# Loads, stores and gate pieces around band attention in a one-core encoder layer: pinned loads in fewer transfers, o and its reciprocals by pairs of heads, gate stores by ScalarE

## The chip, the cores and the metric

The kernel runs on one core of a Trainium2 chip. The metric is the device time of one execution in microseconds (us); lower is better. A core has five engines with instruction streams of their own: TensorE (PE), VectorE (DVE), ScalarE (ACT), GpSimd (POOL) and SyncE (SP), and 16 DMA engines that move data between device memory and the on-chip memory. SP, ACT and POOL each have a queue on which they issue transfers.

## The reference

One layer of a streaming encoder, on 1024 prompt frames and 64 sample frames (1088 columns in all), everything in float32:

```python
proj = xn @ w_in                      # xn = rmsnorm(x); split into cb, cc, ch, q, k, v, ga, gb
cv, conv_state = causal_conv(cc * ch, conv_prefix, w_conv)
ya = (cb * cv) @ w_conv_out
s = einsum('bqhd,bkhd->bhqk', q, k) * HEAD_DIM ** -0.5      # own chunk and 8 chunks before
p = softmax(where(allowed, s + bias, NEG_INF))              # bias by clipped distance, per head
o = einsum('bhqk,bkhd->bqhd', p, v)
yb = o.reshape(B, L, ATT_DIM) @ w_attn_out
merged = sigmoid(ga) * ya + sigmoid(gb) * yb
x = x + merged @ w_out
x = x + (silu(rmsnorm(x) @ w1) * (rmsnorm(x) @ w3)) @ w2    # then a last rmsnorm
```

There are 8 heads of 64. The sample frames attend to 512 cached rows and themselves. New conv state, keys and values are outputs too.

## The kernel before, in words

Every float32 operand is split into a rounded high part and a low part, and a product is three matmuls: high by high, high by low, low by high. The layer runs in stages on TensorE: the projection (to about 377 us of the span), attention with some of the gate projections woven in (to about 555), the remaining gate pieces, the merge (ya, yb, the sigmoids), the output projection, and the feed-forward block. Between stages tensors go through device memory: `q_d`, `k_d` and `v_d` hold q, k and v by head with high and low parts, `ga_d` and `gb_d` the gates, `o_d` the two halves of the attention output before they are added, `rc_d` the reciprocals of the softmax sums, `u_d` the conv branch, `x21_d` a quarter of the normed input that the projection overwrites on chip.

Attention (`attention`, L1016) runs over 8 heads by 9 query tiles t (eight of 128 prompt frames, one of 64 sample frames). A step issues the scores of one tile, the transposes of the tile two steps back, and for pairs of tiles the products with v four steps back. Score tiles are [128, up to 640] in PSUM; VectorE adds the bias and takes the maximum, ScalarE takes the exponent, TensorE transposes, ScalarE and VectorE split into high and low.

Scores need, for a head, q with its high part in both halves of the partitions and likewise its low part (two tiles, L847), and k with high in partitions 0 to 63 and low in 64 to 127 (L851). `head_load` (L844) brings in q in four transfers of 64 partitions, k in four, the bias in four and v in one; `frames_load` (L867) the cached and sample keys `ks` in four and their values `vs` in two. All go out on SP's queue. In the text of the program `head_load(h + 1)` stands at tile 1 of head h and `frames_load(h + 1)` at tile 5, but the scheduler orders what is not pinned by readiness. q, k, v have two buffers, `ks` and `vs` one, the bias two halves of one tile.

`pinned` (L776) fixes the order of an engine's instructions as written. Before the change it is applied to TensorE's matmuls and transposes and to VectorE's and ScalarE's work in attention, not to SP's transfers.

Gates: half of the gate columns are projected here, 32 pieces of 24 matmuls (`gates`, L792). Six run ahead of attention (32 less `WITH` 16 and `BEHIND` 10), 16 are woven into it, 10 run behind it. `GATES` has eight row blocks, `PIECES` four column pieces; pieces 2 and 3 of a block need the quarter that is reloaded from `x21_d` (L1058). A finished piece is copied from PSUM by VectorE into one of two staging tiles and stored by POOL (L810, L811).

At a head's end, `combine` (L879) copies the two halves of p v, adds them on POOL and stores them at `o_d` (L895): 128 partitions go to 2 by 64 rows of device memory. The reciprocals go out at L992 and L996. Behind attention the merge loads the gates of its first row block, u in four blocks, and `o_d` and `rc_d` in four blocks k of two heads (L1067 to L1083); both `o_d` and `rc_d` are one tensor, so the first of these loads waits for the last head's stores. The reciprocals are spread over 64 partitions in two transfers a block.

Of the kernel before, what the change touches and what calls it, by code (L numbers as in the profile page):

```python
# [16 lines left out]
P = 128  # L17
# [20 lines left out]
WITH = 16  # L38
# [27 lines left out]
def encoder_kernel(ctx: ExitStack, tc: tile.TileContext, ins, outs):  # L66
# [33 lines left out]
    o_d = dr.tile([2, ATT, T], F32, name="o_d")  # L100
    rc_d = dr.tile([NH, T], F32, name="rc_d")
# [690 lines left out]
    def gates():  # L792

        kinds = itertools.chain(["att"] * (4 * len(GATES) - WITH - BEHIND), ["mm"] * WITH, turns)
        pieces = [(i, c) for cs in ((0, 1), (2, 3)) for i in range(2) for c in cs]
        pieces += [(i, c) for i in range(2, len(GATES)) for c in range(4)]
        w = {}
        for i, c in pieces:
# [9 lines left out]
            def out(ps=ps, nm=f"gst{i}_{c}", dst=(ga_d if g == "a" else gb_d)[m * P : (m + 1) * P, o : o + n], n=n):  # L808
                st = st_pool.tile([P, HN], F32, tag="st", name=nm)
                tt_copy(st[:, :n], ps[:, :n])  # L810
                nc.gpsimd.dma_start(dst, st[:, :n])  # L811
# [6 lines left out]
    given = [0, False]  # L818
# [24 lines left out]

    def head_load(h):  # L844
        q = []
        for l in range(2):
            qq = hd_pool.tile([P, T], F32R, tag=f"q{l}", name=f"qd{h}_{l}")  # L847
            for j in range(2):
                nc.sync.dma_start(qq[j * HD : (j + 1) * HD].bitcast(F32), q_d[h, :, l])
            q.append(qq)  # L850
        k = hd_pool.tile([P, TP], F32R, tag="k", name=f"kd{h}")  # L851
        v = hd_pool.tile([P, 8, P], F32R, tag="v", name=f"vd{h}")
        halves = [(slice(l * HD, (l + 1) * HD), k_d[h, :, l]) for l in range(2)]
        for e in range(2):
            for ls, src in halves:
                nc.sync.dma_start(k[ls, 512 * e : 512 * e + 512].bitcast(F32), src[:, 576 * e : 576 * e + 512])
# [3 lines left out]
        nc.sync.dma_start(b[:HD, 384:576], near[:HD, :192])  # L860
        nc.sync.dma_start(b[HD:, 384:], near[HD:, :256])
        nc.sync.dma_start(b[:HD, :384], far[:HD])
        nc.sync.dma_start(b[HD:, HD:384], far[HD:, HD:])
        nc.sync.dma_start(v.bitcast(F32), v_d[h, :, :8])
        heads[h] = [q, k, None, v, None, b]

    def frames_load(h):  # L867

        ks = hd_pool.tile([P, CACHE + TS], F32R, tag="ks", name=f"ksd{h}", bufs=1)
        vs = hd_pool.tile([P, 5, P], F32R, tag="vs", name=f"vsd{h}", bufs=1)  # L870
        for l in range(2):
            ls, src = slice(l * HD, (l + 1) * HD), k_d[h, :, l]
# [797 lines left out]
```

## Time and profile before

| | us |
|---|---|
| median of 3 runs | 1520.41 |
| lowest, highest | 1517.18, 1522.82 |
| profiled execution, own time | 1515.17 |
| its span | 1513.4 |
| PE, DVE, ACT, POOL busy | 1464.5, 974.9, 669.0, 186.7 |
| first and last head's first scores start | 396.82, 527.33 |

The span runs from the first to the last instruction of one profiled execution. A group's row has line, engine, operation, target and source tile, shapes, count, busy time and mean; a window's row the busy time of each engine in a stretch. In a row of transfers, KB is the size of one and the last number the median time from issue to landing. Names without numbers stand for all buffers of a tile: `qd` is a head's q tile, `kd` its k, `vd` its v, `ksd` and `vsd` the frames' keys and values, `bb` the bias, `co` the output staged for `o_d`, `gst` a staged gate piece, `g` its PSUM bank, `ob` and `r` the merge's output tiles, `rawp` weights. Lines of several helpers show as L777. q0 is POOL's queue of transfers, q1 SP's.

### The profile page before, as it was taken

How to read it: one execution, taken by the hardware profiler on the slowest of the kernel's cores; microseconds unless marked ns; L12 is line 12 of the kernel's file. 1: busy time of each engine (PE TensorE's matmuls, PEld its weight loads, DVE VectorE, ACT ScalarE, POOL GpSimd, SP SyncE). 2: the span in 40 equal slices, each digit the busy share in tenths (PEclk: the TensorE clock that was granted, in tenths of full speed). 3: DMA queues.
4: the chain of work that ended last, by engine and by line, in shares of the span. 5: the costliest groups of instructions: out<-in, count | busy, mean ns of one | idle time of the engine just before them, and what ended most of it. 6: DMA issues, size and time to landing. Idle time of an engine off the chain costs nothing.

```text
span 1513.4 us, 26409 instructions
## 1 busy us (share of the span) xinstructions
PE 1464.5 (97%) x10130; PEld 1371.1 (91%) x10130; DVE 974.9 (64%) x1815; ACT 669.0 (44%) x1359; POOL 186.7 (12%) x308
## 2 busy tenths in 40 slices
PE   6999999999999998999999999999999999999997
PEld 5799999999988898998888999999999998788886
DVE  6886465464466646763489677666666768857576
ACT  6654433333477761542256444444444445403123
POOL 1210010000265651000100011100001011000000
PEclk9999999999999999999999999999999999999999
DMA  7597523223889867554432434433344448767675
GB/s 232 182 310 241 194 72 108 79 86 135 253 189 200 211 193 235 147 171 148 130 132 84 143 130 157 148 134 119 122 149 157 143 172 314 244 220 229 228 259 202
DMA packets 162334, 264.90 MB, mean 175 GB/s; under 512 B 25536, under 2 KB 95360, under 8 KB 162080
## 3 DMA queue, kind: packets, MB, share of 16 engines
q1 hardware_dynamic: 132848, 196.00, 41.6%
q0 software_dynamic: 28208, 65.12, 12.8%
q10 hardware_dynamic: 1152, 2.10, 0.4%
q8 instruction: 80, 1.31, 0.4%
q14 instruction: 46, 0.38, 0.1%
HBM read 171.06 MB, written 91.92 MB: 174 GB/s over the span
## 4 chain that ended last, share of the span: by engine, by line
PE 63%; issue 20%; DMA 8%; DVE 4%; ACT 1%; SPq 1%; POOL 1%; POOLq 0%; DVEq 0%; ACTq 0%
PE Ab L239 8%; PE Aa L239 8%; PE A L1587 7%; PE Db L239 4%; PE Da L239 4%; PE D L1587 3%; PE Bb L239 2%; PE B L1587 2%; PE g L777 2%; PE Ba L239 2%; DMA kd<-k_d 2%; PE Ak L239 2%; PE Acc L239 2%; PE Ach L239 2%; PE Acb L239 2%
## 5 line engine op out<-in xcount | busy, mean ns | idle before, releaser
L1587 PE MATMUL A<-ring,ht 128*128 128x512 f32 x528 | 126.7, 393 | 3.9 <-ACT acc L1597 2.2
L1587 PEld LDWEIGHTS A<-ring,ht 128*128 128x128 f32 x528 | 98.8, 188 | 27.5 <-ACT acc L1597 3.5
L777 PE MATMUL g<-xn,whp 128*128 128x272 f32 x512 | 104.1, 294 | 2.1 <-DVE gst L777 1.1
L1306 POOL DMA_DIRECT2D h_d<-hq x77 | 41.0, 532 | 415.7 <-DVE hq L123 238.8
L122 ACT CAST ring<-w2r 128x512 fp32r<-128x512 f32 (+1 forms) x78 | 43.6, 587 | 103.7 <-PE A L1587 52.3
L122 ACT CAST hq<-sa 128x512 fp32r<-128x512 f32 x77 | 47.7, 619 | 85.0 <-DVE sa L1318 56.3
L777 PEld LDWEIGHTS g<-xn,whp 128*128 128x128 f32 x512 | 80.9, 188 | 3.8 <-DVE gst L777 1.3
L777 PE MATMUL g<-xn,wlp 128*128 128x272 f32 x256 | 74.6, 292 | 0.0
L123 DVE TENSOR_TENSOR hq<-sa,hq 128x512 fp32r<-128x512 f32 x77 | 53.1, 690 | 32.6 <-ACT hq L122 32.5
L777 DVE CUSTOM_DVE_ANT_0 p<-s,bb 128x640 f32<-128x640 f32 (+5 forms) x72 | 47.8, 664 | 35.7 <-PE s L777 21.5
L123 DVE TENSOR_TENSOR wla<-rawa,wha 128x512 fp32r<-128x512 f32 x56 | 38.5, 687 | 40.5 <-ACT wha L122 40.5
L1587 PE MATMUL D<-ring,ht 128*128 128x512 f32 x264 | 63.9, 393 | 0.2 <-ACT acc L1597 0.2
L239 PE MATMUL Aa<-tt,wha 128*128 128x272 f32 x352 | 58.9, 288 | 2.7 <-ACT tt L122 2.5
L1587 PEld LDWEIGHTS D<-ring,ht 128*128 128x128 f32 x264 | 49.5, 188 | 12.0 <-ACT acc L1597 0.6
L239 PE MATMUL Ab<-mg,whb 128*128 128x272 f32 x352 | 58.4, 288 | 0.0
L239 PE MATMUL Aa<-mg,wha 128*128 128x272 f32 x352 | 58.3, 288 | 0.0
L239 PE MATMUL Ab<-tt,whb 128*128 128x272 f32 x352 | 58.2, 287 | 0.0
L302 PE MATMUL yb<-ob,whp 128*128 128x272 f32 x256 | 50.8, 295 | 7.4 <-ACT ob L122 5.6
L122 ACT CAST wha<-rawa 128x512 fp32r<-128x512 f32 x56 | 34.8, 621 | 51.2 <-PE Ab L239 35.2
L123 DVE TENSOR_TENSOR ring<-w2r,ring 128x512 fp32r<-128x512 f32 (+1 forms) x78 | 49.1, 646 | 12.0 <-ACT ring L122 11.8
L239 PEld LDWEIGHTS Aa<-tt,wha 128*128 128x128 f32 x352 | 49.6, 188 | 3.4 <-ACT tt L122 2.9
L777 ACT ACTIVATE p<-p,mx 128x640 f32<-128x640 f32 (+5 forms) x72 | 51.0, 708 | 3.7 <-DVE mx L777 3.0
(542 smaller groups left out, 4312.1 us busy)
## 6 DMA issues: line engine op xcount, KB each, us to landing
h_d<-hq POOLq DMA_DIRECT2D x77, 512.0 KB, 3.4
ht<-h_d SPq DMA_DIRECT2D x154, 256.0 KB, 3.7
rawa<-in_w_ff SPq DMA_DIRECT2D x11, 1024.0 KB, 5.8
rawb<-in_w_ff SPq DMA_DIRECT2D x11, 1024.0 KB, 5.4
w2r<-in_w_ff SPq DMA_DIRECT2D x11, 1024.0 KB, 5.7
qd<-q_d SPq DMA_DIRECT2D x32, 272.0 KB, 7.4
ga<-ga_d SPq DMA_DIRECT2D x32, 136.0 KB, 2.6
gb<-gb_d SPq DMA_DIRECT2D x32, 136.0 KB, 2.4
```

Source lines behind the costliest of these rows:

```text
L122: act.copy(hi, src)
L123: vec.tensor_tensor(lo, src, hi.bitcast(F32), op=ALU.subtract)
L239: mm(t[:, j, :HN], w[:, k, :], x[p][:, l, k, j * HN : (j + 1) * HN], start=p in (1, 2, 7) and k == 0 and n == 0, stop=k == 3 and n == 2, s ...
L302: mm(out, l, r, start=k + j == 0, stop=k == kt - 1 and j == 2)
L777: return lambda *a, **kw: pin(f(*a, **kw))
L1306: nc.gpsimd.dma_start(h_d[p, c - 1], hq.rearrange("p i l t -> p (i l t)").bitcast(F32))
L1587: mm(t, ht[k][:, j, x], w[:, l], start=p in (1, 2, 7) and k == 0 and n == 0, stop=k == len(ks) - 1 and n == 2, skip_group_check=p in (6, 5 ...
```

## The change

Five things, all around attention:

- The heads' loads are pinned in the order of the program on SP's queue, and so is the reload from `x21_d`, which now stands between head 0's q, k and bias and its v.
- They are fewer: q is one tile [128, 2, 1088] loaded by one transfer whose source repeats the head's rows (step 0, count 2) for the two halves of the partitions; k is loaded in two transfers and `ks` in two, with high and low (step TK, count 2) as the outermost dimension of the source. `values_load` and `frame_values_load` stand apart: frames' keys of head h and q, k, bias of head h + 1 go at tile 1, frames' values of h and v of h + 1 at tile 5.
- `o_d` and `rc_d` are four tensors each, one for each pair of heads; the merge's loads of a pair and of u are interleaved, and a pair's reciprocals come in one transfer with the head (step T, count 2) outermost.
- Gate pieces behind attention are copied and stored by ScalarE.
- Four gate pieces go ahead of attention in place of six, 18 with it, and the first three row blocks give their pieces 0 and 1 first.

```diff
 C_CB, C_CC, C_CH, C_Q, C_K, C_V, C_GA, C_GB = 0, 512, 1024, 1536, 2048, 2560, 3072, 4096
-WITH = 16
+WITH = 18
 BEHIND = 10
...
     gb_d = dr.tile([D, T], F32, name="gb_d")
-    o_d = dr.tile([2, ATT, T], F32, name="o_d")
-    rc_d = dr.tile([NH, T], F32, name="rc_d")
+    o_d = [dr.tile([2, P, T], F32, name=f"o_d{k}") for k in range(4)]
+    rc_d = [dr.tile([2, T], F32, name=f"rc_d{k}") for k in range(4)]
...
         kinds = itertools.chain(["att"] * (4 * len(GATES) - WITH - BEHIND), ["mm"] * WITH, turns)
-        pieces = [(i, c) for cs in ((0, 1), (2, 3)) for i in range(2) for c in cs]
-        pieces += [(i, c) for i in range(2, len(GATES)) for c in range(4)]
+        pieces = [(i, c) for cs in ((0, 1), (2, 3)) for i in range(3) for c in cs]
+        pieces += [(i, c) for i in range(3, len(GATES)) for c in range(4)]
         w = {}
...
                 st = st_pool.tile([P, HN], F32, tag="st", name=nm)
-                tt_copy(st[:, :n], ps[:, :n])
-                nc.gpsimd.dma_start(dst, st[:, :n])
+                if behind[0]:
+                    act.copy(st[:, :n], ps[:, :n])
+                    nc.scalar.dma_start(dst, st[:, :n])
+                else:
+                    tt_copy(st[:, :n], ps[:, :n])
+                    nc.gpsimd.dma_start(dst, st[:, :n])
...
     gate_products = gates()
-    given = [0, False]
+    given, behind = [0, False], [False]
...
+    load_at = pinned(nc.sync.dma_start)
+
+    def rows_of(src, *ap):
+        return bass.AP(tensor=src.tensor, offset=src.offset, ap=[list(d) for d in ap])
+
     def head_load(h):
-        q = []
-        for l in range(2):
-            qq = hd_pool.tile([P, T], F32R, tag=f"q{l}", name=f"qd{h}_{l}")
-            for j in range(2):
-                nc.sync.dma_start(qq[j * HD : (j + 1) * HD].bitcast(F32), q_d[h, :, l])
-            q.append(qq)
-        k = hd_pool.tile([P, TP], F32R, tag="k", name=f"kd{h}")
-        v = hd_pool.tile([P, 8, P], F32R, tag="v", name=f"vd{h}")
-        halves = [(slice(l * HD, (l + 1) * HD), k_d[h, :, l]) for l in range(2)]
+        q = hd_pool.tile([P, 2, T], F32R, tag="q", name=f"qd{h}")
+        load_at(q.bitcast(F32), rows_of(q_d[h], (0, 2), (2 * T, HD), (T, 2), (1, T)))
+        k = hd_pool.tile([P, 2, 512], F32R, tag="k", name=f"kd{h}")
         for e in range(2):
-            for ls, src in halves:
-                nc.sync.dma_start(k[ls, 512 * e : 512 * e + 512].bitcast(F32), src[:, 576 * e : 576 * e + 512])
+            load_at(k[:, e].bitcast(F32), rows_of(k_d[h, :, 0, 576 * e :], (TK, 2), (2 * TK, HD), (1, 512)))
         b = bb[:, h % 2]
...
         far = bias_rows(h, 0, 384)
-        nc.sync.dma_start(b[:HD, 384:576], near[:HD, :192])
-        nc.sync.dma_start(b[HD:, 384:], near[HD:, :256])
-        nc.sync.dma_start(b[:HD, :384], far[:HD])
-        nc.sync.dma_start(b[HD:, HD:384], far[HD:, HD:])
-        nc.sync.dma_start(v.bitcast(F32), v_d[h, :, :8])
-        heads[h] = [q, k, None, v, None, b]
+        load_at(b[:HD, 384:576], near[:HD, :192])
+        load_at(b[HD:, 384:], near[HD:, :256])
+        load_at(b[:HD, :384], far[:HD])
+        load_at(b[HD:, HD:384], far[HD:, HD:])
+        heads[h] = [q, k.rearrange("p e t -> p (e t)"), None, None, None, b]
+
+    def values_load(h):
+        v = heads[h][3] = hd_pool.tile([P, 8, P], F32R, tag="v", name=f"vd{h}")
+        load_at(v.bitcast(F32), v_d[h, :, :8])
...
-        ks = hd_pool.tile([P, CACHE + TS], F32R, tag="ks", name=f"ksd{h}", bufs=1)
-        vs = hd_pool.tile([P, 5, P], F32R, tag="vs", name=f"vsd{h}", bufs=1)
-        for l in range(2):
-            ls, src = slice(l * HD, (l + 1) * HD), k_d[h, :, l]
-            nc.sync.dma_start(ks[ls, :CACHE].bitcast(F32), src[:, T:])
-            nc.sync.dma_start(ks[ls, CACHE:].bitcast(F32), src[:, 512:576])
-        nc.sync.dma_start(vs[:, :4].bitcast(F32), v_d[h, :, 8:12])
-        nc.sync.dma_start(vs[:TS, 4].bitcast(F32), v_d[h, :TS, 12])
-        heads[h][2], heads[h][4] = ks, vs
+        ks = heads[h][2] = hd_pool.tile([P, CACHE + TS], F32R, tag="ks", name=f"ksd{h}", bufs=1)
+        for c, src, n in ((0, k_d[h, :, 0, T:], CACHE), (CACHE, k_d[h, :, 0, 512:], TS)):
+            load_at(ks[:, c : c + n].bitcast(F32), rows_of(src, (TK, 2), (2 * TK, HD), (1, n)))
+
+    def frame_values_load(h):
+        vs = heads[h][4] = hd_pool.tile([P, 5, P], F32R, tag="vs", name=f"vsd{h}", bufs=1)
+        load_at(vs[:, :4].bitcast(F32), v_d[h, :, 8:12])
+        load_at(vs[:TS, 4].bitcast(F32), v_d[h, :TS, 12])
...
             pool_e.tensor_tensor(o[:, :n], a[:, 0, :n], a[:, 1, :n], op=ALU.add)
-            to = o_d[:, h * HD : (h + 1) * HD]
+            to = o_d[h // 2][:, h % 2 * HD : (h % 2 + 1) * HD]
             spans = [((tok if tok < 512 else HT + tok - 512), 0, n)]
...
                 mm_at(
-                    ps[:, i], q[l][:, q0 : q0 + r], k[:, k0 + i * w : k0 + i * w + w], start=l == 0, stop=l == 1
+                    ps[:, i], q[:, l, q0 : q0 + r], k[:, k0 + i * w : k0 + i * w + w], start=l == 0, stop=l == 1
                 )
...
                     nc.gpsimd.dma_start(
-                        rc_d[h, e * HT : e * HT + 512].rearrange("(t p) -> t p", p=P), rows[4 * e : 4 * e + 4]
+                        rc_d[h // 2][h % 2, e * HT : e * HT + 512].rearrange("(t p) -> t p", p=P), rows[4 * e : 4 * e + 4]
                     )
                     c = e * HT + 512
-                    nc.gpsimd.dma_start(rc_d[h : h + 1, c : c + 32], rows[8:9, 32 * e : 32 * e + 32])
+                    nc.gpsimd.dma_start(rc_d[h // 2][h % 2 : h % 2 + 1, c : c + 32], rows[8:9, 32 * e : 32 * e + 32])
...
                 h, t = order[i]
-                if t == 1 and h + 1 < NH:
-                    head_load(h + 1)
-                elif t == 5 and h + 1 < NH:
-                    frames_load(h + 1)
+                if t == 1:
+                    frames_load(h)
+                    if h + 1 < NH:
+                        head_load(h + 1)
+                elif t == 5:
+                    frame_values_load(h)
+                    if h + 1 < NH:
+                        values_load(h + 1)
                 done.append(scores(h, t))
...
     head_load(0)
-    frames_load(0)
-
-    nc.sync.dma_start(xn.t[0, 1].rearrange("p l k t -> p (l k) t").bitcast(F32), x21_d)
+
+    load_at(xn.t[0, 1].rearrange("p l k t -> p (l k) t").bitcast(F32), x21_d)
+    values_load(0)
     gate(24 * (4 * len(GATES) - WITH - BEHIND), False)
...
     sg = gates_in(0)
-    for k in range(4):
+
+    def o_load(k):
+        rc, o2 = (ob.t[:, l, k].bitcast(F32) for l in range(2))
+        r = mp.tile([P, T], F32, tag="rc", name=f"r{k}", bufs=2)
+        nc.sync.dma_start(r, o_d[k][0])
+        nc.sync.dma_start(o2, o_d[k][1])
+        nc.sync.dma_start(rc, rows_of(rc_d[k], (T, 2), (0, HD), (1, T)))
+        vec.tensor_tensor(r, r, o2, op=ALU.add)
+        vec.tensor_tensor(r, r, rc, op=ALU.mult)
+        split(ob.t[:, 0, k], ob.t[:, 1, k], r)
+
+    def u_load(k):
         f = u.t[:, 1, k].bitcast(F32)
...
         split(u.t[:, 0, k], u.t[:, 1, k], f)
-    for k in range(4):
-        rc, o2 = (ob.t[:, l, k].bitcast(F32) for l in range(2))
-        r = mp.tile([P, T], F32, tag="rc", name=f"r{k}", bufs=2)
-        nc.sync.dma_start(r, o_d[0, k * P : (k + 1) * P])
-        nc.sync.dma_start(o2, o_d[1, k * P : (k + 1) * P])
-        for j in range(2):
-            src = rc_d[2 * k + j]
-            nc.sync.dma_start(
-                rc[j * HD : (j + 1) * HD], bass.AP(tensor=src.tensor, offset=src.offset, ap=[[0, HD], [1, T]])
-            )
-        vec.tensor_tensor(r, r, o2, op=ALU.add)
-        vec.tensor_tensor(r, r, rc, op=ALU.mult)
-        split(ob.t[:, 0, k], ob.t[:, 1, k], r)
+
+    o_load(0)
+    u_load(0)
+    o_load(1)
+    for k in range(1, 4):
+        u_load(k)
+    o_load(2)
+    o_load(3)
+    behind[0] = True
     gate(24 * 4 * len(GATES), False)
```

## The prediction, made before the change was timed

> **What bounds the kernel now.** I read the page first (span, busy shares, chain), then a table by windows over the stage that the change touches, then the waits, and last the transfers of that stage. From the page:
>
> ```profile
> span 1513.4 us, 26409 instructions
> PE 1464.5 (97%) x10130; PEld 1371.1 (91%) x10130; DVE 974.9 (64%) x1815; ACT 669.0 (44%) x1359; POOL 186.7 (12%) x308
> PE 63%; issue 20%; DMA 8%; DVE 4%; ACT 1%; SPq 1%; POOL 1%; POOLq 0%; DVEq 0%; ACTq 0%
> ```
>
> TensorE is busy 97% of the span, so at most 49 us stand open in the whole kernel, and this change removes no matmul. The windows show attention (397 to 545), the gate pieces behind it (560 to 590) and the start of the merge (600 to 612). Columns: us, busy of PE, weight loads, DVE, ACT, POOL, granted clock, share of the 16 DMA engines, GB/s.
>
> ```profile
> 397.00:472.00 75.00, 69.39 (x499) 64.09 (x499) 50.04 (x125) 56.17 (x135) 39.03 (x57) 1.00 0.85 204
> 472.00:491.00 19.00, 18.27 (x131) 16.89 (x130) 11.73 (x30) 14.35 (x35) 10.84 (x16) 1.00 0.90 199
> 560.00:590.00 30.00, 30.00 (x241) 30.00 (x240) 15.17 (x20) 10.30 (x16) 6.23 (x11) 1.00 0.70 220
> 600.00:606.00 6.00, 1.12 (x8) 0.91 (x8) 2.58 (x2) 0.82 (x1) 0.00 (x0) 0.97 0.82 210
> 606.00:612.50 6.50, 6.12 (x25) 5.80 (x26) 6.19 (x14) 4.00 (x10) 0.00 (x0) 0.50 0.21 60
> ```
>
> In attention TensorE is nearly full, but so are the transfers: the DMA engines hold packets 85 to 90% of the time. Every head reloads its q, k, v and bias tiles while the head before runs, so this stage has two bounds that lie close together, and what the change does to the loads decides it. The waits tell what loads and stores cost today (us in total, times, longest):
>
> ```profile
> PE s L777 <- DMA kd<-k_d: 6.4, 5, 2.3
> PE yb L302 <- ACT ob L122: 5.6, 2, 5.2
> SPq L1074 <- DMA o_d<-co_s: 8.2, 1, 8.2
> DVE gst L777 <- DMA gb_d<-gst: 12.9, 5, 4.1
> ```
>
> **What the change can win.** Scores wait 6.4 us for k; an order that is fixed on SP's queue could take that to zero. The merge waits 5.6 us for ob, after which the clock is granted at 0.50 for 6.5 us (the last window), which is 3.2 us of work lost; o_d in one tensor for each pair of heads lets the first three pairs load before the last head has been stored (the 8.2 us), which could remove both. That is 15.2 us. ScalarE in place of VectorE and POOL for the 10 gate pieces behind attention takes away the 12.9 us in which VectorE waits for a staging buffer, but in 560 to 590 TensorE is busy 30.00 of 30 us: nothing gained there, and ScalarE, busy 10.30 of 30, has room for ten copies and issues. What is queued behind each on ScalarE are the next weight casts and the splits of u and ob. Two gate pieces that move from ahead of attention into it add no work; they cost the cover of the first head's loads, below.
>
> **What the change costs.** The merged loads have the same bytes, and here is the step on which I decide. Before, q came in four loads of 64 partitions each, k in four, the frames' keys in four. Now one load has a source access pattern whose outermost dimension is 2: (0,2) for q, which is the two copies, and (TK,2) for k and ks, which is hi and lo. The reciprocals of the merge get (T,2). The trace of before has one transfer with such a pattern, the o_d store at L895, whose target is 2 by 64 rows. The first two lines below are a stretch in which that store alone moves data on POOL's queue (q0); the next two a stretch with a h_d store on the same queue, 128 rows on both sides:
>
> ```profile
> DMA packets 66, 0.03 MB, mean 42 GB/s; under 512 B 58, under 2 KB 58, under 8 KB 66
> q0 software_dynamic: 66, 0.03, 17.0%
> ...
> DMA packets 162, 0.54 MB, mean 287 GB/s; under 512 B 14, under 2 KB 34, under 8 KB 162
> q0 software_dynamic: 142, 0.52, 90.3%
> ```
>
> 17.0% of 16 engines is 2.7 engines, against 14.4 for the h_d store: the 2 by 64 store runs at 42 GB/s on about two engines, with the other fourteen empty. I take the same for the four merged loads, on SP's queue. The nearest row is this store; it is another queue and a store, so that stays the largest doubt (rivals). The Trainium skill, page "DMA: Bandwidth & Descriptors", section "Why a DMA increments its semaphore by 16 and not by 1", states that on either kind of queue a transfer uses the largest number of engines up to 16 that divides the slowest dimension of both sides, and that on SP's and ACT's these are the lowest-numbered; the store agrees with its 42 GB/s, and no run here shows it for SP. The same page, in "Rules for kernel authors", also advises one transfer of 128 partitions in place of two of 64, which is what the change does, and by that rule alone the sum would be the first rival's.
>
> Sizes and times now. The loads (KB each, us to landing), and a stretch in which large loads alone fill all engines:
>
> ```profile
> qd<-q_d SPq DMA_DIRECT2D x32, 272.0 KB, 7.4
> kd<-k_d SPq DMA_DIRECT2D x32, 128.0 KB, 6.5
> ksd<-k_d SPq DMA_DIRECT2D x16, 128.0 KB, 7.5
> ksd<-k_d SPq DMA_DIRECT2D x16, 16.0 KB, 7.5
> rawp<-in_w_in SPq DMA_DIRECT2D x4, 1024.0 KB, 5.3
> xn<-x_d SPq DMA_DIRECT2D x1, 2176.0 KB, 10.2
> u<-u_d SPq DMA_DIRECT2D x4, 544.0 KB, 9.4
> r<-o_d SPq DMA_DIRECT2D x4, 544.0 KB, 4.6
> ob<-o_d SPq DMA_DIRECT2D x4, 544.0 KB, 6.8
> ob<-rc_d SPq DMA_DIRECT2D x8, 272.0 KB, 7.9
> ...
> DMA packets 324, 0.81 MB, mean 407 GB/s; under 512 B 122, under 2 KB 141, under 8 KB 324
> ```
>
> 407 GB/s over 16 is 25.4 GB/s for one engine; the store's 42 over two is 21. Both are kept as ends, and I take 25.4, since loads of 2 KB and more are what it was read from. For each head, one of the two engines then carries:
> - q: 4 x 272 KB = 1.114 MB, half of it 557 kB, 21.9 us
> - k: 4 x 128 KB = 0.524 MB, half 262 kB, 10.3 us
> - ks: 2 x (128 + 16) KB = 0.295 MB, half 147 kB, 5.8 us
> - its sixteenth of all else: window 472 to 491 is one head and moves 199 GB/s x 19 us = 3.78 MB; less the 1.93 MB above, 1.85 MB over 16 is 116 kB, 4.5 us
>
> The sum is 42.5 us for a head. A head lasts 18.6 us now: first scores of head 0 at 396.82, of head 7 at 527.33, a seventh of the difference.
>
> ```profile
> 377.85 0.52 PE L777 MATMUL g<-xn,whp 128*128 128x272 f32 x2 [1.03 <-ACT scr L531]
> 378.72 1.79 SPq L849 DMA_DIRECT2D qd<-q_d  x1
> 396.82 0.34 PE L777 MATMUL s<-kd,qd 128*128 128x128 f32 x2
> 527.33 0.42 PE L777 MATMUL s<-kd,qd 128*128 128x128 f32 x2 [1.74 <-DMA kd<-k_d]
> 555.65 2.35 SPq L1069 DMA_DIRECT2D u<-u_d  x4
> ```
>
> Buffers don't hide that: q, k and v have two, so head h+1's loads may go out a head ahead, but the two engines carry 42.5 us of packets for every head whatever the lead. The pinned order adds to it that everything behind q and k on the queue (bias, values, the gates' weights) has a sixteenth of its packets waiting on the same two engines, and TensorE, whose order is pinned too, can't go round a late score. So:
> - Head 0: 378.7, 1.8 to issue, 2.6 for the weight load in front (1024 KB over 16), 21.9 and 10.3: scores at 415.3, 18.5 later than now. The gate pieces ahead are four from 377.85 on, of 24 matmuls each; window 560 to 590 has 241 in 30.00 us, so 3.0 us a piece: they end near 390 and cover none of the stop.
> - Head 1: 42.5 more, and 5.5 for x21 (2176 KB over 16), which is pinned behind head 0's loads: 463.3.
> - Heads 2 to 7: 6 x 42.5, so head 7 at 718.3 in place of 527.3: plus 191.0 us. SP's waits for free buffers (scores of the head before, its values) lie inside the 42.5, as TensorE is then ahead of the loads.
> - Head 7's own work follows a long stop. Going by the 606 window it runs 6.5 us at half clock: plus 3.2. In the heads before it that loss is hidden by the loads.
> - The merge: uo opens at about 555.65 as now. One of the two engines carries half of the reciprocals' 8 x 272 KB, 1.114 MB, 43.9 us, and a sixteenth of 12 loads of 544 KB (u, r, o2), 16.4 us: all landed at 616.0. Then VectorE multiplies, ScalarE rounds and VectorE subtracts over 1088 columns, 2.1 times the 690, 619 and 690 ns of 512 columns in the two rows below, some 4 us: ob is whole at 620, where TensorE goes on at 606 now: plus 14 us. The gate pieces cover it up to about 590 only, and ya up to 596. The 15.2 us to be won are gone: the waits they sit in are replaced by longer ones.
>
> ```profile
> L122 ACT CAST hq<-sa 128x512 fp32r<-128x512 f32 x77 | 47.7, 619 | 85.0 <-DVE sa L1318 56.3
> L123 DVE TENSOR_TENSOR hq<-sa,hq 128x512 fp32r<-128x512 f32 x77 | 53.1, 690 | 32.6 <-ACT hq L122 32.5
> ```
>
> 191.0 + 3.2 + 14 = 208.2 us. The profiled execution took 1515.17 us (its span 1513.4) and lies 5.2 under the median of 1520.41; 1515.2 + 208.2 + 5.2 = 1729 us. With 21 GB/s for an engine the head costs 51.5 us and the whole comes to 1813; with all else hidden a head costs 38.0 and the whole comes to 1697. This case's own range is 1690 to 1800.
>
> **The rivals.**
> 1. *The merged loads spread over all 16 engines* as the 64-row loads do now. Then bytes and rate are as before, SP has seven issues fewer for each head, and the 15.2 us come in as far as the stops allow: 1515.2 - 15.2 + 5.2 = 1505 us, faster. For it: the store of 42 GB/s is on another queue, and no SP transfer of before has an outermost 2. Against it: the engines are handed out by the shape of the pattern in the one place where it can be seen. It decides as soon as a merged q load lands in under 10 us.
> 2. *Two engines, but another pair for each transfer.* Then q's 21.9 us set the pace alone, k and ks run beside it: with 18.6 us of lead and about 2 us to issue and land, some 5 us of stop for each of six heads, and 8 for head 0: 1515.2 + 38 + 5.2 = 1558 us, the merge unchanged. For it: two o_d stores that overlapped in the trace moved 66 GB/s together, as in this stretch:
>
> ```profile
> DMA packets 80, 0.10 MB, mean 66 GB/s; under 512 B 57, under 2 KB 57, under 8 KB 80
> q0 software_dynamic: 80, 0.10, 24.0%
> ```
>
> so POOL's stores can take different pairs. Against it: that is POOL's queue, whose descriptors POOL writes; for SP's queue no row shows a change of engines, and I give it little.
>
> **How the numbers follow.** My case 0.82, rival 1 0.13, rival 2 0.05. The range is my case's own, 1690 to 1800, which leaves out its tails and both rivals: a little under 2 in 10. About 0.5% is what a measurement of this kernel can tell from no change. Rival 1 is 1.0% faster, with little chance of ending within 0.5%: faster 0.12, same 0.01. Both others are slower: 0.87.
>
> **What would show it.** Right, if the merged q load takes over 20 us to land, the DMA engines' share in attention falls to about 0.3 while TensorE idles some 24 us in each head (released by the loads of q and k), heads start about 42 us apart, and the merge's reciprocals take more than 10 us each. Wrong, if q lands in about 7 us, the DMA share stays at 0.85, and heads stay 18 to 19 us apart; then rival 1 holds. Heads about 23 us apart would be rival 2. A price off in size alone would show as a head spacing between 38 and 52.

## The result and the profile after

| | before | after |
|---|---|---|
| median, us | 1520.99 (1517.18 to 1522.82, 5 runs) | 1763.76 (1761.54 to 1766.85, 5 runs) |
| ratio | | 1.160, 95% interval 1.158 to 1.162 |
| span of the profiled execution | 1513.4 | 1762.4 |
| first scores of heads 0, 1, 7 | 396.8, 413.3, 527.3 | 412.2, 463.2, 734.2 |
| last matmul of attention | 555.38 | 767.93 |

The change makes the kernel 16% slower, 243 us by the medians and 249.0 us by the two spans. From the page of the changed kernel, the span, TensorE's busy time, and three rows of the slices (each digit is the busy share of a fortieth of the span, in tenths; GB/s is left out):

```profile
span 1762.4 us, 26310 instructions
PE 1499.8 (85%) x10130; PEld 1402.3 (80%) x10130; DVE 972.4 (55%) x1805; ACT 672.7 (38%) x1369; POOL 180.8 (10%) x298
...
PE   7999999984454544493899999999999999899998
...
PEclk9999999996676767797899999999999999999999
DMA  7695432243222322354454433433334334875776
```

The same 10130 matmuls run, at 85% in place of 97%. A slice is 44 us, and the tenth to the seventeenth are attention: there TensorE is busy 40 to 50% at a clock of 0.6 to 0.7, and the DMA engines stand at 20 to 30%, where the windows of before had 85 to 90%. Both bounds of the stage stand idle together, so something holds it back by a part of a resource: here, as the transfers below show, by few of the sixteen engines. The groups (busy us, mean ns of one | idle us ahead of them and what ended it) show who waits:

```profile
L777 PE MATMUL s<-kd,qd 128*128 128x320 f32 (+2 forms) x192 | 43.4, 337 | 180.2 <-DMA kd<-k_d 180.2
L302 PE MATMUL ya<-u,whp 128*128 128x272 f32 x256 | 53.5, 303 | 18.6 <-ACT u L122 15.0 <-DVE u L123 2.1 <-ACT gst L811 1.5
L302 PE MATMUL yb<-ob,whp 128*128 128x272 f32 x256 | 52.3, 302 | 14.8 <-ACT ob L122 14.1 <-DVE ob L123 0.7
```

The wait for k was 6.4 us in all before; now it is 180.2, eight times, the longest 26.7. The timeline of TensorE in the changed kernel (start, us, [idle before <- releaser]) has the stops ahead of the first, second and last head, and the last matmul of attention:

```profile
412.25 0.66 PE L777 MATMUL s<-kd,qd 128*128 128x128 f32 x2 [20.51 <-DMA kd<-k_d]
463.24 0.66 PE L777 MATMUL s<-kd,qd 128*128 128x128 f32 x2 [26.67 <-DMA kd<-k_d]
...
734.23 0.66 PE L777 MATMUL s<-kd,qd 128*128 128x128 f32 x2 [22.28 <-DMA kd<-k_d]
...
767.93 0.28 PE L777 MATMUL pv<-ident,sm 128*9 128x128 f32 x1
```

From 412.25 to 734.23 are seven heads: 46.0 us each, where it was 18.6 (45.2 without the first of the seven steps, in which the reload from `x21_d` stands). In the kernel before, the last line's instruction stands here:

```profile
555.38 0.28 PE L777 MATMUL pv<-ident,sm 128*9 128x128 f32 x1
```

So the 249.0 us fall into three: up to head 7's first scores 734.2 - 527.3 = 206.9; head 7's own work (767.93 - 734.23) - (555.38 - 527.33) = 5.6; and all behind attention (1762.4 - 767.93) - (1513.4 - 555.38) = 36.4.

What holds the heads is seen in the transfers of the changed kernel while one q load runs (524.7 to 547.3; packets and MB, then SP's queue q1: packets, MB, share of 16 engines):

```profile
DMA packets 913, 1.58 MB, mean 70 GB/s; under 512 B 669, under 2 KB 677, under 8 KB 785
...
q1 hardware_dynamic: 131, 1.10, 12.0%
```

12.0% of sixteen engines is 1.92: as much as two engines that hardly rest, and fourteen with nothing from SP. They move 1.10 MB in 22.6 us, 48.7 GB/s, or 24.3 GB/s each. The loads go one after the other. In the head before, `ks` and q were both issued by 471.92; the first packet of q (8704 bytes, two rows) comes at 478.0, behind the last of `ks`. SP's queue while `ks` alone has packets (472 to 476.5), and while k alone has, behind q (548 to 551):

```profile
q1 hardware_dynamic: 107, 0.22, 12.6%
...
q1 hardware_dynamic: 73, 0.15, 13.0%
```

Again that is two engines' worth, in the first window with q waiting in line. The order of the queue alone doesn't make q wait: as soon as the bias, which has no count of 2, is issued behind k, it runs beside it, and from 551 to 553 SP's queue holds 47.1%. SP's own timeline around that load (start, us, operation) shows the second half of the story:

```profile
512.57 1.10 SPq L777 DMA_DIRECT2D ksd<-k_d  x2
513.71 1.67 SPq L777 DMA_DIRECT2D qd<-q_d  x1
515.43 29.52 SPq L777 DMA_DIRECT2D kd<-k_d  x2
545.04 5.84 SPq L777 DMA_DIRECT2D bb<-bias_d  x2
```

The two k loads take SP 29.52 us to issue, with no releaser named. In each of heads 1 to 7 these issues end 2.9 to 3.3 us before the last packet of q, whatever their length (23.0 to 29.5 us), so it looks as if SP stands until the two engines have drained most of q. The bias of the next head is issued only then, and VectorE's first work on the scores waits for it (195.8 us in seven waits, in the time in which TensorE waits for k).

In the merge the same thing happens once more, with the reciprocals. SP's issues there, VectorE's waits for the reciprocals (us in total, times, longest), ScalarE's casts behind the first and second reciprocals, and the stops of TensorE that follow:

```profile
777.20 0.32 SPq L1079 DMA_DIRECT2D r<-o_d  x1
...
779.06 0.53 SPq L1081 DMA_DIRECT2D ob<-rc_d  x1
779.64 0.73 SPq L1088 DMA_DIRECT2D u<-u_d  x1
...
783.87 1.16 SPq L1081 DMA_DIRECT2D ob<-rc_d  x1
789.62 10.77 SPq L1088 DMA_DIRECT2D u<-u_d  x3
```

```profile
DVE r L1083 <- DMA ob<-rc_d: 41.8, 4, 11.1
```

```profile
798.14 1.10 ACT L122 CAST ob<-r 128x1088 fp32r<-128x1088 f32 x1 [13.77 <-DVE r L1083]
...
815.19 1.10 ACT L122 CAST ob<-r 128x1088 fp32r<-128x1088 f32 x1 [6.97 <-DVE r L1083]
816.20 1.09 ACT L122 CAST u<-u 128x1088 fp32r<-128x1088 f32 x1
```

```profile
817.34 0.60 PE L302 MATMUL ya<-u,whp 128*128 128x272 f32 x1 [15.01 <-ACT u L122]
835.96 0.60 PE L302 MATMUL yb<-ob,whp 128*128 128x272 f32 x1 [7.26 <-ACT ob L122]
```

u's last three loads stand behind two pairs of o and reciprocals on SP's queue, and on ScalarE the cast of u's second block stands right behind that of ob's second block, which waits, by way of VectorE, for the second reciprocals. So ya, which needs no reciprocal at all, stops 15.01 us for u, and yb then 7.26 and 6.85.

### The profile page after: what moved, and what is told of

It is laid out like the page before. It is cut to its first block, busy times and chain, and to the rows that moved or that the text cites. A ratio compares the mean times of both kernels' runs of the same rounds, so it can differ in the third digit from the quotient of the medians.

```text
span 1762.4 us, 26310 instructions
## 1 busy us (share of the span) xinstructions
PE 1499.8 (85%) x10130; PEld 1402.3 (80%) x10130; DVE 972.4 (55%) x1805; ACT 672.7 (38%) x1369; POOL 180.8 (10%) x298
## 5 line engine op out<-in xcount | busy, mean ns | idle before, releaser
L777 PE MATMUL s<-kd,qd 128*128 128x320 f32 (+2 forms) x192 | 43.4, 337 | 180.2 <-DMA kd<-k_d 180.2
L777 DVE CUSTOM_DVE_ANT_0 p<-s,bb 128x640 f32<-128x640 f32 (+5 forms) x72 | 47.7, 664 | 250.5 <-DMA bb<-bias_d 195.8
L777 PEld LDWEIGHTS s<-kd,qd 128*128 128x128 f32 x192 | 32.7, 209 | 181.7 <-issue 181.7
L777 PE MATMUL g<-xn,whp 128*128 128x272 f32 x512 | 110.7, 306 | 1.5 <-ACT scr L531 1.0
L777 ACT CAST pt<-t 128x640 fp32r<-128x640 f32 (+2 forms) x64 | 35.7, 558 | 181.8 <-PE t L777 181.0
L777 PEld LDWEIGHTS g<-xn,whp 128*128 128x128 f32 x512 | 87.0, 201 | 3.3 <-ACT scr L531 1.2
L302 PE MATMUL ya<-u,whp 128*128 128x272 f32 x256 | 53.5, 303 | 18.6 <-ACT u L122 15.0
L302 PE MATMUL yb<-ob,whp 128*128 128x272 f32 x256 | 52.3, 302 | 14.8 <-ACT ob L122 14.1
L777 PE MATMUL t<-ident,p 128*128 128x128 f32 (+1 forms) x280 | 45.7, 289 | 17.0 <-DVE mx L777 11.2
L302 PEld LDWEIGHTS ya<-u,whp 128*128 128x128 f32 x256 | 43.4, 201 | 20.2 <-ACT u L122 15.2
```

The source lines that it names most:

```text
L302: mm(out, l, r, start=k + j == 0, stop=k == kt - 1 and j == 2)
L777: return lambda *a, **kw: pin(f(*a, **kw))
```

## The experiments

Theory: a transfer whose pattern has an outermost count of 2 runs on two engines, the same two for every such load on SP's queue, and that is the whole loss. Rivals: the loss comes from something else in the change (the pinned order, merging as such, o ahead of u, ScalarE's stores); or each such transfer has two engines of its own. Each of e1, e5 to e12 was timed beside the kernel before on the same chip; e2 to e4 are single executions (the kernel before had 1524.40 there).

**e1: the changed kernel, but all its merged loads in halves of 64 rows.**

```diff
-        load_at(q.bitcast(F32), rows_of(q_d[h], (0, 2), (2 * T, HD), (T, 2), (1, T)))
+        for j in range(2):
+            load_at(q[j * HD : (j + 1) * HD].bitcast(F32), q_d[h])
```

(k, `ks` and the reciprocals likewise.)

> The changed kernel with one thing undone: the four kinds of merged loads (q, k, ks, the reciprocals) go out in transfers of 64 rows again, so that no source has an outermost dimension of 2. Pins, order, o and reciprocals by pairs, ScalarE's gate stores and four pieces ahead all stay. Theory (two engines carry a transfer whose outermost dimension is 2): heads fall back from 46 to 18 or 19 us apart, the DMA share in attention rises to 0.85, and the time is about 1505 us, 1495 to 1515. Rival (the pinned order on SP's queue, or ScalarE's stores behind its casts, is what costs): heads stay over 25 us apart or the merge keeps its stops, and the time stays over 1560 us.

Measured: 1526.67 us against 1524.40, ratio 1.0019 (1.0003 to 1.0035); heads 20.0 us apart (two more woven gate pieces among them), and no stop for k over 1 us. The loss is gone, so it was in the merged loads; whether in the merging or in the count of 2, e9 tells. The gain that was hoped for (1505 us) did not come: the waits of this kernel have a stop for u in place of most of the old one for ob.

```profile
ACT co_s L777 <- DMA o_d<-co: 11.7, 3, 4.3
...
PE ya L302 <- ACT u L122: 4.7, 1, 4.7
...
PE yb L302 <- ACT ob L122: 2.3, 1, 2.3
```

(us in total, times, longest.) ya stops 4.7 us for u where yb's longest for ob was 5.2 before, and ScalarE waits three times for an o_d store, which is still one of 2 by 64 rows.

**e2: as e1, but the reciprocals of a pair in one transfer again.**

```diff
-        for j in range(2):
-            nc.sync.dma_start(rc[j * HD : (j + 1) * HD], rows_of(rc_d[k][j], (0, HD), (1, T)))
+        nc.sync.dma_start(rc, rows_of(rc_d[k], (T, 2), (0, HD), (1, T)))
```

> As the kernel with loads of 64 rows, but the merge's reciprocals are still one transfer for a pair of heads, with the head (count 2) outermost. Theory: attention is as with 64 rows, and the merge has four transfers of about 11 us one after the other on the same two engines, with u behind them: 25 to 35 us over the kernel with 64 rows, some 1535 us. If each transfer gets a pair of engines of its own, the four run side by side and the time is within 8 us of the kernel with 64 rows.

Measured: 1564.68, 38.0 over e1. The waits of the changed kernel's merge come back by themselves:

```profile
PE ya L302 <- ACT u L122: 14.7, 1, 14.7
PE yb L302 <- ACT ob L122: 14.5, 2, 7.5
```

Four transfers of 544 KB cost the whole loss of the merge, 3 us over the upper end of what was expected.

**e3: the kernel before, with q merged and nothing else; e4: the kernel before, with k and `ks` merged and nothing else.** Neither is pinned.

```diff
-            for j in range(2):
-                nc.sync.dma_start(qq[j * HD : (j + 1) * HD].bitcast(F32), q_d[h, :, l])
...
+            q.bitcast(F32), bass.AP(tensor=s.tensor, offset=s.offset, ap=[[0, 2], [2 * T, HD], [T, 2], [1, T]])
```

```diff
-            for ls, src in halves:
-                nc.sync.dma_start(k[ls, 512 * e : 512 * e + 512].bitcast(F32), src[:, 576 * e : 576 * e + 512])
...
+                bass.AP(tensor=s.tensor, offset=s.offset, ap=[[TK, 2], [2 * TK, HD], [1, 512]]),
...
```

> The kernel before with one edit: q comes in one transfer whose source has the two copies outermost; k, ks, order and all else as before, nothing pinned. Theory: the two engines carry q (22 to 23 us) and a sixteenth of the other 2.67 MB of a head (6.6 us), so heads are 29 to 30 us apart in place of 18.6, and the time is some 1600 us (1585 to 1620). Rival (another pair for each transfer): q alone must land in a head's 18.6 us, heads 22 to 24 us apart, 1550 to 1565 us. Rival (spread over 16): 1520 us.

> The kernel before with one edit: k in two transfers and ks in two, with high and low (count 2) outermost; q in four as before, nothing pinned. Theory: two engines carry k (10.3 us), ks (5.8 to 10) and a sixteenth of the other 2.96 MB (7.3 us): heads 23.5 to 27.5 us apart, 1560 to 1590 us. Rival (another pair for each transfer): no transfer takes over 6 us, all of it is hidden in the 18.6 us, 1520 to 1525 us.

Measured: e3 1645.75 us, heads 33.6 apart; e4 1613.94, heads 31.1 apart. Both cost more than expected, by 26 us over the upper end for e3 and 24 for e4, and more than their packets were reckoned at on two engines. For e3 the trace shows a part of it: a head's q took 23.9 to 27.2 us in place of 22 to 23, and for 6.6 to 12.8 us the two engines then carried no q, since the next one stands on SP's queue behind loads of k and of the frames' values, whose issues waited 46.8 and 54.0 us, in three stops each, until a q had landed. In e4 SP's timeline shows at least that loads which have no count of 2 there, those of q and of the bias, take long to issue (5.91 us for four, 6.72 us for one), which fits a queue that stands while two engines carry k and `ks`:

```profile
438.30 5.91 SPq L849 DMA_DIRECT2D qd<-q_d  x4
...
466.89 6.72 SPq L863 DMA_DIRECT2D bb<-bias_d  x1
473.71 5.75 SPq L874 DMA_DIRECT2D ksd<-k_d  x2
```

The three parts nearly add up. Against their own base, q costs 121.4 us, k and `ks` 89.5, the reciprocals 38.0: 248.9 in all, and the changed kernel stands 1763.76 - 1526.67 = 237.1 over e1. As e3 and e4 cost more than was reckoned, the nearness of the two sums is in part luck. Engines of their own for each transfer are ruled out otherwise: e4 would then have cost nothing (1520 to 1525 us were expected for that case), and in the changed kernel SP's queue holds two engines' worth for `ks` (12.6%) while q, already issued, waits in line, so they share the two.

**e5: as e1, but the gate pieces behind attention copied by VectorE and stored by POOL. e6: as e1, but without the pins on SP's loads.**

```diff
-    behind[0] = True
```

```diff
-    load_at = pinned(nc.sync.dma_start)
+    load_at = nc.sync.dma_start
```

> The kernel with loads of 64 rows, and the gate pieces behind attention copied by VectorE and stored by POOL again. In the run with 64 rows ScalarE waited 6.2 and 5.6 us for a staging tile whose store had not landed, with the casts of ob and u queued behind it, and ya then stopped 4.7 us for u. Theory (the staging wait was moved to the engine that u needs): the 4.7 us stop goes, 3 to 6 us faster than with ScalarE, some 1522 us. Rival (u is late because its loads stand behind the o loads): the stop stays and the time is within 2 us.

> The kernel with loads of 64 rows, SP's loads not pinned. Theory (the pinned order is worth nothing that can be measured once loads are wide, since waits for k were 6.4 us in all before): within 4 us of the pinned one, either way, and waits of the scores for k come back. Rival (the pin is worth the 6.4 us): 5 to 8 us slower. Rival (the pin holds v back behind the frames' values, as the pinned run's stops before the products with v suggest): 3 to 6 us faster.

Measured: e5 1525.95 against 1523.70, ratio 1.0005 (0.9986 to 1.0024), the stop for u 3.6 us; e6 1526.23, 1.0018 (1.0000 to 1.0035), with one stop of 4.6 us ahead of scores. Neither part moves the time by what a measurement can tell: the gate stores on ScalarE were not what held u, and the theory of e5, 3 to 6 us faster, falls. ScalarE's order may well have done so, which no run shows by itself: in e5 too u's casts stand right behind that of ob's second block.

```profile
593.59 1.10 ACT L122 CAST ob<-r 128x1088 fp32r<-128x1088 f32 x1 [9.08 <-DVE r L1088]
594.60 3.10 ACT L122 CAST u<-u 128x1088 fp32r<-128x1088 f32 x3
```

**e7: the kernel before, with the o_d store as two of 64 rows. e8: e1 with the same.**

```diff
-                nc.gpsimd.dma_start(to[:, :, c : c + w], o[:, e : e + w])
+                for l in range(2):
+                    nc.gpsimd.dma_start(to[l, :, c : c + w], o[l * HD : (l + 1) * HD, e : e + w])
```

> The kernel before with one edit: each store to o_d goes out as two transfers of 64 rows, in place of one of 2 by 64. Theory (count 2 outermost means two engines, on POOL's queue as on SP's): the store's own stretch moves over 100 GB/s in place of 42 to 66, and the time falls by 0 to 4 us, since few wait for these stores. Rival (POOL's descriptors are the limit, not the engines): the rate stays at 40 to 60 GB/s and the time rises by up to 5 us for the 48 more issues.

> The kernel with loads of 64 rows, and the o_d stores as two transfers of 64 rows. There ScalarE waited 11.7 us for an output tile whose o_d store had not landed, and TensorE stopped 2 to 3 us three times behind it. Theory: those stops go, 4 to 8 us faster than with the 2 by 64 stores, some 1519 us. Rival (the store is late for POOL's sake): no change or 2 us slower.

Measured: e7 1517.65 against 1523.70, ratio 0.9954 (0.9938 to 0.9970); e8 1521.13, 0.9975 (0.9956 to 0.9995). The one such transfer that the kernel always had cost it 0.46%. The transfers of before, then of e7 (KB each, median us to landing), both on POOL's queue:

```profile
o_d<-co POOLq DMA_DIRECT2D x32, 128.0 KB, 7.2
```

```profile
o_d<-co POOLq DMA_DIRECT2D x64, 64.0 KB, 3.4
```

Twice as many issues land in about half the time each, and in e7 heads are 17.2 us apart in place of 18.6, with no wait for k left.

**e9: e8, with k_d laid out as [head, high or low, 64, TK], so that a k load is one transfer of 128 rows with an outermost count of 128 (`ks` likewise; the stores into k_d follow the new layout).**

```diff
-    k_d = dr.tile([NH, HD, 2, TK], F32, name="k_d")
+    k_d = dr.tile([NH, 2, HD, TK], F32, name="k_d")
...
-            for l in range(2):
-                load_at(k[l * HD : (l + 1) * HD, e].bitcast(F32), k_d[h, :, l, 576 * e : 576 * e + 512])
+            load_at(k[:, e].bitcast(F32), k_d[h].rearrange("l d t -> (l d) t")[:, 576 * e : 576 * e + 512])
```

> The kernel of e8 with k_d laid out as [head, high/low, 64, TK], so that a k load (two a head) and a load of the frames' keys (two a head) is one transfer of 128 partitions again, as in the change, but with an outermost dimension of 128 in place of 2; q stays in two loads of 64 rows. Theory (the count of 2 outermost is what costs, not the merging): heads 18 to 19.5 us apart, no stop for k over 3 us, 1516 to 1526 us beside the 1521 of e8. Rival (a merged load to 128 partitions costs by itself, by its size or the way it is issued): the 31.06 us a head of e4, over 1590 us.

Measured: 1519.74 against 1523.55, ratio 0.9977 (0.9962 to 0.9992); heads 18.5 us apart. Its k loads (KB each, us to landing):

```profile
kd<-k_d SPq DMA_DIRECT2D x16, 256.0 KB, 9.3
```

The same 256 KB into the same 128 partitions in one transfer is harmless when the count of 2 isn't outermost; it also brings nothing over e8's two halves. This is the cleanest proof, for k and `ks`: a merged load to the same partitions, without the 2 outermost. For q, whose two copies come from a step of 0, no such run was made; there the evidence is e3 and the two engines while it runs.

**e10: e7, with o_d and rc_d by pairs and nothing else of the change.**

```diff
-        nc.sync.dma_start(r, o_d[0, k * P : (k + 1) * P])
-        nc.sync.dma_start(o2, o_d[1, k * P : (k + 1) * P])
+        nc.sync.dma_start(r, o_d[k][0])
+        nc.sync.dma_start(o2, o_d[k][1])
...
```

> The kernel of e7 (the kernel before, with the o_d stores as two of 64 rows) and of the change only that o_d and rc_d are one tensor for each pair of heads; the order of the merge's loads stays (u first, then o), the reciprocals in two loads of 64 rows. Theory 1 (the ob stop of before is there only because the first o load waits for the last head's store, and in the change it was ya's stop for u that took its place, as o was put ahead of u): PE's stops for ob, 2.4, 1.3 and 4.1 us in e7, go below 2 us together, and 3 to 8 us come off: 1510 to 1515 us. Theory 2 (another wait ends last in the same place: the chain add, multiply, round, subtract of ob on VectorE and ScalarE, or the loads' rate): the stops stay within 3 us of e7's, 1515 to 1520 us.

Measured: 1515.47 against 1523.55, ratio 0.9950 (0.9933 to 0.9967), that of e7. The stops for ob stay, 2.4 and 3.4 us: theory 1 of this run falls. SP's timeline in e10 points to another cause:

```profile
565.91 0.61 SPq L1075 DMA_DIRECT2D r<-o_d  x1
...
584.30 0.33 SPq L1075 DMA_DIRECT2D r<-o_d  x1
...
590.20 0.33 SPq L1075 DMA_DIRECT2D r<-o_d  x1
```

The third and fourth blocks go out 18 and 24 us behind the second, each just behind the subtraction that frees one of the two staging tiles `r`. In e7, with one o_d for all heads, these issues stand at 567.79, 584.56 and 590.46: with stores of 64 rows the last head no longer holds the merge, pairs or not, and these two buffers of 1088 columns do, which e12 tests.

**e11: e8, with u loaded ahead of o, as before.**

```diff
-    o_load(0)
-    u_load(0)
-    o_load(1)
-    for k in range(1, 4):
-        u_load(k)
-    o_load(2)
-    o_load(3)
+    for k in range(4):
+        u_load(k)
+    for k in range(4):
+        o_load(k)
```

> The kernel of e8, but with the merge's loads in the order of the kernel before: u's four blocks first, then o and the reciprocals by pairs. In e8 ya stops 1.4 and 1.9 us for u and yb 2.4 us for ob; in e10, which loads u first, ya does not stop and yb stops 2.4 and 3.4 us. Theory (the order only moves the stop: what is loaded first is ready, what is loaded behind it is late by as much): ya's stops below 1 us, yb's up to 5 to 7 us together, 1518 to 1523 us beside the 1521 of e8. Rival (u first removes ya's stops and adds none): 3 to 5 us come off, 1515 to 1518 us.

Measured: 1523.54 against 1521.67, ratio 1.0006 (0.9991 to 1.0020). ya's stops are gone and yb's are longer (PE's waits of e11):

```profile
PE yb L302 <- ACT ob L122: 7.1, 2, 3.7
...
PE ya L302 <- ACT gst L811: 0.3, 1, 0.3
```

The order of u and o only says which of the two is late. By their ratios e11 lies 0.3% over e8, and the two intervals overlap.

**e12: e10, with the merge's o worked in two halves of the columns and four staging tiles of half the size.**

```diff
-    for k in range(4):
-        rc, o2 = (ob.t[:, l, k].bitcast(F32) for l in range(2))
-        r = mp.tile([P, T], F32, tag="rc", name=f"r{k}", bufs=2)
+    for e in range(2):
+        c = slice(e * HT, e * HT + HT)
+        for k in range(4):
+            rc, o2 = (ob.t[:, l, k, c].bitcast(F32) for l in range(2))
+            r = mp.tile([P, HT], F32, tag="rc", name=f"r{k}_{e}", bufs=4)
...
```

> The kernel of e10, but with the merge's o and reciprocals worked in two halves of the 1088 columns (first all four blocks of one half, then those of the other) and four staging tiles r of half the size in place of two. In e10 the third and fourth r load go out at 584.30 and 590.20 us, each just after the subtraction that frees one of the two r tiles (it starts at 582.98 and 588.88), and ob's last cast is at 600.25. Theory (the two r tiles hold ob back, so that yb stops 2.4 and 3.4 us for it): the first half of ob is ready before yb starts, the stops go below 2 us together, and 3 to 6 us come off: 1510 to 1513 us. Rival (VectorE and ScalarE, which do the same columns in twice the instructions beside the gates' copies and the sigmoids, are what is late): stops within 2 us of those of e10, 1514 to 1517 us.

Measured: 1510.07 against 1521.67, ratio 0.9913 (0.9895 to 0.9932), the fastest of all. One stop for ob is left:

```profile
PE yb L302 <- ACT ob L122: 1.9, 1, 1.9
```

Against e10 that is 0.37% less by the ratios, 5.6 us, of which the stops explain 5.7 - 1.9 = 3.8. More buffers and smaller pieces came together here; which of the two did it is not shown.

## Why the prediction was right, point by point

The forecast was 1729 us, in a range of 1690 to 1800; measured were 1763.76. Both its cause and its sign hold; its sizes were low in three terms.

1. *Two engines for an outermost count of 2, on SP's queue too.* Right: 1.92 engines while q runs, 24.3 GB/s each between the 21 and 25.4 that were kept as ends, and e9, in which a merged load without the 2 outermost costs nothing. The signs that were named came: q took over 20 us, the DMA share in attention was 0.30 (412.2 to 734.2), TensorE stopped 20.0 to 26.7 us ahead of each head, and VectorE waited up to 11.1 us for a pair's reciprocals. The Trainium skill, page "DMA: Bandwidth & Descriptors", states in the section "Why a DMA increments its semaphore by 16 and not by 1" that the slowest dimension sets the number of engines, and that SP's are always the lowest-numbered; the trace agrees with the first by that 1.92. That the two engines are the same for every such load is shown by q waiting behind `ks` and k behind q; which of the sixteen they are, no run here shows. Rival 1 (all sixteen) and rival 2 (another pair for each) are both out.
2. *42.5 us for a head.* Head 0 came at 412.2 (forecast 415.3). That head 1 came at 463.2 (463.3) is luck: the step between them was 51.0 us in place of 48.0, and the two misses cancel. The six behind took 45.2 us each: 206.9 up to head 7 in place of 191.0. By its packets a head's q took 22.6 to 25.3 us, 23.4 in the mean of heads 2 to 7, in place of 21.9: that is 557 kB at 23.8 GB/s for each of the two engines, not 25.4. The stretch between two q, in which k, `ks` and the forecast's "sixteenth of all else" go, took 21.8 us in the mean, in place of 20.6. So the engine's rate was the larger miss. `ks`, forecast at 5.8 us, took 6.4 to 7.0 in four heads and about 10 in two, among them the one from 514.4 to 524.7; there SP's share fell to 5.3% between 518 and 522 while POOL's queue held 19.4%. That the two met on the same engines would explain it, but the profile doesn't number the engines.
3. *Head 7 after its stop: 3.2.* 5.6: the window from its first scores to its last matmul grants a clock of 0.92 (34 us x 0.08 = 2.7), TensorE stops once more for 1.4 us, and some gate matmuls more fall into it. The two windows of the changed kernel on which this and the next point rest (columns as in the prediction):

```profile
734.00:768.00 34.00, 32.27 (x217) 29.94 (x217) 15.39 (x39) 17.21 (x41) 15.71 (x23) 0.92 0.45 121
...
800.00:850.00 50.00, 17.75 (x85) 15.64 (x85) 16.84 (x17) 8.04 (x12) 0.00 (x0) 0.65 0.41 133
```

4. *The merge: 14.* 36.4, the largest miss of a single term. The stops of ya and yb are 26.0 us longer by the groups' rows (18.6 and 14.8, against 7.4 for yb alone before), and the matmuls of ya and yb take 7.5 us more, at a clock of 0.65 from 800 to 850; 2.9 are spread. The step that failed is "ya up to 596": it took u as loaded. The change puts u's second to fourth load behind two pairs of o and reciprocals, these three issues take SP 10.77 us, and u's cast stands behind ob's on ScalarE. The prediction costed the slow reciprocals, not what is queued behind them. The three terms are short by 15.9, 2.4 and 22.4 us, 40.7 together. The forecast also added 5.2 us, the distance of the profiled execution of before from its median, which the changed kernel's (1764.18, median 1763.76) doesn't have; 40.7 - 5.2 = 35.5 is about the 34.8 by which 1729 missed. The range was drawn from the engine's rate and the overlap alone; that it also held a merge 22.4 us longer is slack, not reckoning.
5. *15.2 us to be won, that the stops would eat.* That they did not come is right, but rival 1, which pays them out in full, was wrong beyond its premise: with these loads in halves of 64 rows (e1) the ratio is 1.0019, not 0.990. The wait for k went with the o_d store's two engines (e7), without any pin; the stop for ob, once the store was split, hung on the staging tiles (e10, e12; their number or their size), not on the shared `o_d`, and o ahead of u turned part of it into one for u (e11).
6. *Gates by ScalarE, nothing gained.* Right (e5). The pin on the loads, which the prediction thought worth up to 6.4 us, is worth nothing that can be measured either (e6).

A rule spoke against the forecast. The Trainium skill, page "DMA: Bandwidth & Descriptors", section "Rules for kernel authors", advises one transfer of 128 partitions in place of two of 64. Here the measurement decides against it where the merged pattern has the 2 outermost (1763.76 against 1526.67), and finds no difference where it has 128 (e9 against e8). The same list's advice to put a multiple of 16 outermost is what e9 bears out.

## What to carry to other kernels

Before two loads are merged into one, look at the outermost count of the merged pattern, not at the bytes or partitions: here a leading 2, from two copies or from high and low, left two engines at work, and everything that was queued behind them waited. In a profile the sign was a stage in which TensorE and the DMA engines fell idle together, with a queue's share at about two sixteenths (12.0 to 13.0%). When a wait goes, find what holds the resource behind it before counting the gain: here the stop for ob had two holders, stores and staging tiles, and taking away the first alone left the stop as it was.

## What the runs showed of the hardware that was not expected

- SP itself stands, as it looks until the two engines have drained most of what is in front of them: 29.52 us for two issues, 10.77 us for three, with no releaser in the profile; the issues of k end 2.9 to 3.3 us before q's last packet. Loads without the count of 2 wait behind it just as well (those of the bias are issued only then).
- Transfers with a count of 2 on SP's queue go one after the other across tensors: q's first packet comes 6.1 us after its issue ended, when `ks` is through, and the queue's share is 12.0 to 13.0% in the windows in which one of these loads runs alone. e3 and e4 each cost 24 to 26 us over the upper end that was expected from the sizes; that surplus is explained in part for e3 and stays open for e4.
- A store of 128 KB on two engines costs even a kernel in which it looks hidden: 0.46% (e7), though none of TensorE's waits in the kernel before names it. How much of that is tiles that wait for the store (ScalarE in e1, 11.7 us) and how much its packets on two engines, the runs don't separate.
- The profile gives no landing time for any of SP's transfers in the changed kernel; a queue's share of the sixteen engines, in a window where it runs alone, takes its place.
